# One product for o and v in head groups 2 and 3: seven block products where there were eight

## The chip, the cores and the metric

The kernel runs on one core of a Trainium2 chip. The metric is the device time of one execution in microseconds (us). The core has a matrix engine (TensorE, PE in the profile, with its weight loads as PEld), a vector engine (VectorE, DVE), a scalar engine (ScalarE, ACT), GpSimd (POOL), and SyncE (SP), which here only issues transfers. Each engine works through its own list of instructions in order, and semaphores join the lists.

## The reference, cut to what matters

Two layers work on 256 tokens of 2048 channels; the part below is one layer. Everything is float32.

```python
u = rms_norm(x, norm_g)
p = u @ w_in                                   # 256 x 2048 by 2048 x 12304
qk, v, o, z_a, ig, fg, xb, z_b = split(p)
qk = silu(causal_dwconv(qk, qk_conv))          # a convolution over time, 4 taps
h = mlstm_chunkwise(q, k, v, i_pre, log_f)     # 8 heads of 256
h = h * sigmoid(o);  h = normalise(h) * head_norm_g
y_a = h * silu(z_a)
xc = causal_dwconv(xb, lru_conv_w) + lru_conv_b
y_b = rg_lru(xc) * silu(z_b)                   # gates by two small products, then a scan over time
x = x + concat([y_a, y_b]) @ w_out
```

## The kernel before

**Tiles.** Per layer there are four head groups g of two heads, 512 channels of each kind. The weights lie in memory as units of 1 MB (128 partitions by 2048 float32), in the order in which they are used. A unit has two halves of 128x1024. Each half is split into two numbers of fewer bits, H and L: ScalarE casts it to wH (line 309), VectorE subtracts to get wL (line 310, through the helper at line 178). The activations are kept split in the same way (`x_s`). A float32 product is then three matmuls, HH, HL and LH, which go into one PSUM sum.

- For o, v, z and the output product (`mm_a`, lines 325 to 327) the activation is stationary, a weight row of 512 moves, and a half is 12 matmuls of 512 columns.
- For qk, xb and zb (`mm_b`, lines 342 and 344) the weight is stationary, and a half is 8 matmuls of 512 and 8 of 256 columns.

**Order.** `_sequence()` writes down the order of the units. For a group g from 1 on, it is a head (four units of o, four of v; with zb of group 0 between them in g = 1) and a body: qk, two chunks of the output product of g-1, xb, two more chunks, z, gate, zb. That is 25 units in a body. A running half n prepares (`prepare`) up to half n + `AHEAD` (3), and the pools wH and wL hold four halves (`bufs=4`): so the cast of half n+4 waits until TensorE is done with half n.

**Between the units.** When a PSUM sum is complete, its `..._post` empties it: `evac_b` for qk, xb and zb (a copy on ScalarE, line 416, then an add on VectorE that reads the same sum, line 417), `postfn` of `out_chunk` for the output product (line 799), `o_post`, `v_post`, `z_post`. The rest of the work (convolutions, attention, gates, scan) lies in generators in the queue `bg`, and `pump` hands out some of it after each half. Sums lie in two pairs of PSUM banks, `acc0` and `acc1`, used in turn, so one fills while the other is emptied. Four more banks (`aux0`, `aux1`, two buffers each) serve the small products: attention `ps_S`, `ps_n`, gates `ps_gt`, transposes `ps_ty`. A scheduler in the compiler then shifts instructions inside each engine's list.

**Loading.** `load_unit` takes one buffer of 128x2048 from a pool of three (`wraw`, line 99), and SyncE issues one transfer of 1 MB (line 286) as soon as the buffer's last reader is done.

**What is there but not in use.** The functions `sw_forms`, `sw_chunk` and `sw_post` compute o and v of one group as one product of 2x2 blocks with 7 block products (the Winograd form of Strassen's scheme), in two parts, B (3 block products) and A (4). The set `SW` (line 32) is empty in the kernel before, so none of this runs, and neither does the staging at lines 1033 to 1046 and 1071 to 1077.

Of the kernel before, what the change touches and what calls it, by code (L numbers as in the profile page):

```python
# [9 lines left out]
F32 = mybir.dt.float32  # L10
F32R = mybir.dt.float32r
AF = mybir.ActivationFunctionType
ALU = mybir.AluOpType
# [3 lines left out]
P = 128  # L17
# [11 lines left out]
STAGE_FROM, STAGE_EVERY = 12, 2  # L29


SW = set()
# [6 lines left out]
def _sequence():  # L39


    def units(item):
        return [(item, j) for j in range(_nunits(item))]

    def spread(items, extra):
        groups = []
        for it in items:
            u = units(it)
            groups += [u[i : i + 2] for i in range(0, len(u), 2)]
        side = [x for it in extra for x in units(it)]  # L50
# [24 lines left out]
    return seq  # L75
# [18 lines left out]
def tile_trunk(ctx, tc, x, xt, par, gw, gb, ws, final_g, out):  # L94
# [4 lines left out]
    wraw = ctx.enter_context(tc.tile_pool(name="wraw", bufs=3))  # L99
# [77 lines left out]
    def tt_(o, a, b, op):  # L177
        return V.tensor_tensor(out=o, in0=a, in1=b, op=op)  # L178
# [75 lines left out]
    seq, blocks, pq = _sequence(), _blocks(), {}  # L254

    def sw_blocks(item, kp):

        u = [ws[blocks[("in", item[1], k, item[2]), kp // 2]] for k in "ov"]
        o = 1024 * (kp % 2)
        return [[w[:, o + 512 * r : o + 512 * r + 512] for w in u] for r in range(2)]  # L260

    def load_unit(n, item, j):
        raw = wraw.tile([P, 2048], F32, tag="raw", name="raw")
        st["nload"] += 1
        u = blocks.get((item, j))
        if item[0] == "swB":
            even, odd = sw_blocks(item, j)
            nc.sync.dma_start(out=raw[:, 0:512], in_=even[0])
            nc.sync.dma_start(out=raw[:, 512:1024], in_=odd[1])
            nc.sync.dma_start(out=raw[:, 1024:1536], in_=pq[item[1:]][j][:, 0:512])  # L270
            return raw
        if item[0] == "swA":
            uo = blocks[("in", item[1], "o", item[2]), j // 2]
            nc.sync.dma_start(out=raw[:, 0:1024], in_=ws[uo][:, 1024 * (j % 2) : 1024 * (j % 2) + 1024])
            nc.sync.dma_start(out=raw[:, 1024:1536], in_=pq[item[1:]][j][:, 512:1024])
            tt_(raw[:, 0:512], raw[:, 0:512], raw[:, 1024:1536], ALU.add)
            tt_(raw[:, 1536:2048], raw[:, 0:512], raw[:, 512:1024], ALU.add)
            return raw
        if n < 4:
            w = 512 if n == 0 else 1024  # L280
            for o in range(0, 2048, w):
                if o % 1024 == 0:
                    load_xt(n, o // 1024)
                nc.sync.dma_start(out=raw[:, o : o + w], in_=ws[u][:, o : o + w])
        else:
            nc.sync.dma_start(out=raw, in_=ws[u])
        return raw
# [6 lines left out]
    def prepare(hf):  # L294
        n = len(xT_parts) if hf["i"] == 0 else 1
        if hf["i"] == 0:
            hf["box"]["raw"] = load_unit(n, *hf["at"])
            if n < 4:
                split_xT(0, n, xT_parts[n], range(4 * n, 4 * n + 4))
            if 4 <= st["nload"] < 8:  # L300
                load_x(st["nload"] - 4)
        r = hf["box"]["raw"][:, 1024 * hf["i"] : 1024 * hf["i"] + 1024]
# [235 lines left out]
    def v_post(l, g, acc):  # L538
# [12 lines left out]
        bg.append(e_gen(l, g))  # L551
# [307 lines left out]
    def sw_chunk(l, g, which):  # L859
# [14 lines left out]
        for kp in range(8):  # L874
# [6 lines left out]
            add_unit(mms, before=sw_banks if kp == 0 else None,  # L881
                     after=(lambda: sw_post(l, g, which)) if kp == 7 else None,
                     width=(1024, 512 if which == "B" else 1024))

    def sw_post(l, g, which):
        m = st["sw"]["banks"]
        st["sw"] = None
        if which == "B":
# [4 lines left out]
            st["credit"] -= 1.3  # L893
            return
        require(("lru", l, g - 1))
        require(("ybT", l, g - 1))
        e = st["swe"]
        t = work.tile([P, 512], F32, tag="sC", name="swt")
        tt_(t, e[:, 0, :], m[1], ALU.add)
        tt_(e[:, 0, :], e[:, 0, :], m[0], ALU.add)  # L900
        tt_(e[:, 1, :], e[:, 1, :], m[1], ALU.subtract)
        tt_(e[:, 2, :], e[:, 2, :], m[1], ALU.subtract)
        tt_(t, t, m[2], ALU.add)
        tt_(e[:, 1, :], e[:, 1, :], m[2], ALU.subtract)
        tt_(t, t, m[3], ALU.add)
        st["credit"] -= 4.8
        o_post(l, g, (e[:, 0, :], t))
        v_post(l, g, (e[:, 2, :], e[:, 1, :]))
# [9 lines left out]
    def emit_in(l, kind, g):  # L918
        def first_gen(acc):
# [15 lines left out]
            if SW:  # L935
                yield from sw_forms(l)

        posts = {"o": o_post, "v": v_post, "qk": qk_post, "xb": xb_post, "z": z_post, "zb": zb_post}
# [94 lines left out]
    staged = []  # L1033
    for item, j in seq:
        if item[0] == "swB":
            d = dram.tile([P, 1024], F32, name=f"pq{item[1]}{item[2]}{j}")
            pq.setdefault(item[1:], []).append(d)
            staged.append((d, sw_blocks(item, j)))

    def stage_copy(d, b):  # L1040
        for h in range(2):
            S.dma_start(out=d[:, 512 * h : 512 * h + 512], in_=b[0][1])

    def stage_add(d, b):
        for h in range(2):
            G.dma_start(out=d[:, 512 * h : 512 * h + 512], in_=b[h][h], accum_op=ALU.add)

# [19 lines left out]
    for n, hf in enumerate(order_):  # L1067
# [3 lines left out]
        if hf["i"] == 0:  # L1071
            k = (n // 2 - STAGE_FROM) // STAGE_EVERY
            if n // 2 >= STAGE_FROM and (n // 2 - STAGE_FROM) % STAGE_EVERY == 0:
                if k < len(staged):
                    stage_copy(*staged[k])
                if 0 < k <= len(staged):
                    stage_add(*staged[k - 1])
# [103 lines left out]
```

## Time and profile before

| | |
|---|---|
| time, median of 3 runs (lowest to highest) | 1528.44 us (1528.32 to 1528.78) |
| the profiled execution's own time | 1528.54 us |
| its span, first to last instruction | 1526.8 us |
| TensorE busy | 1509.5 us, 99% of the span |
| VectorE busy | 1077.9 us, 71% |
| ScalarE busy | 891.4 us, 58% |
| GpSimd busy | 62.7 us, 4% |
| moved by DMA | 309 MB, 202 GB/s on average |

The page gives for each engine the time in which an instruction of it ran. Matmuls overlap: one is listed with 390 ns, and the next starts 227 ns later. So what a number of matmuls costs is read from the length of a stretch divided by their count, not from the listed durations. In the same way a VectorE instruction may begin a little before the last one ends.

A steady group, from the first matmul of its o to the first matmul of the next group's o, takes 186.53 us (344.41 to 530.94), of which the head is 43.56 us and the body 142.97 us.

### The profile page before, as it was taken

How to read it: one execution, taken by the hardware profiler on the slowest of the kernel's cores; microseconds unless marked ns; L12 is line 12 of the kernel's file. 1: busy time of each engine (PE TensorE's matmuls, PEld its weight loads, DVE VectorE, ACT ScalarE, POOL GpSimd, SP SyncE). 2: the span in 40 equal slices, each digit the busy share in tenths (PEclk: the TensorE clock that was granted, in tenths of full speed). 3: DMA queues.
4: the chain of work that ended last, by engine and by line, in shares of the span. 5: the costliest groups of instructions: out<-in, count | busy, mean ns of one | idle time of the engine just before them, and what ended most of it. 6: DMA issues, size and time to landing. Idle time of an engine off the chain costs nothing.

```text
span 1526.8 us, 19954 instructions
## 1 busy us (share of the span) xinstructions
PE 1509.5 (99%) x7704; PEld 1284.5 (84%) x7704; DVE 1077.9 (71%) x1510; ACT 891.4 (58%) x1151; POOL 62.7 (4%) x136
## 2 busy tenths in 40 slices
PE   8999999999999999999999999999999999999997
PEld 6888888888888888888888888888888888888885
DVE  6887866676666856758658786676857759477584
ACT  6667554574555745548655485555845557455564
POOL 0010100000000000000001010000000000000002
PEclk9999999999999999999999999999999999999999
DMA  9654556755566555775655545566555665566753
GB/s 357 235 190 174 198 188 209 218 177 198 187 220 202 185 193 193 230 241 192 222 191 179 194 172 195 191 203 218 193 193 183 205 219 193 190 198 219 247 202 102
DMA packets 52926, 309.02 MB, mean 202 GB/s; under 512 B 5712, under 2 KB 8288, under 8 KB 19552
## 3 DMA queue, kind: packets, MB, share of 16 engines
q1 hardware_dynamic: 45776, 287.59, 52.0%
q0 software_dynamic: 4448, 15.75, 6.1%
q10 hardware_dynamic: 2608, 4.42, 0.8%
q8 instruction: 60, 0.98, 0.2%
q14 instruction: 34, 0.28, 0.1%
HBM read 288.85 MB, written 18.89 MB: 202 GB/s over the span
## 4 chain that ended last, share of the span: by engine, by line
PE 97%; DVE 1%; ACT 1%; DMA 0%; issue 0%; ACTq 0%; SPq 0%
PE acc L342 23%; PE acc L325 18%; PE acc L327 18%; PE acc L326 18%; PE acc L344 12%; PE ps_gt L693 3%; PE acc_x L976 0%; PE acc L974 0%; PE acc_x L974 0%; PE acc_x L975 0%; PE acc L976 0%; PE acc L975 0%; PE ps_n L524 0%; PE ps_ty L647 0%; PE ps_n L526 0%; PE ps_n L525 0%
## 5 line engine op out<-in xcount | busy, mean ns | idle before, releaser
L178 DVE TENSOR_TENSOR wL<-raw,wH 128x1024 fp32r<-128x1024 f32 (+1 forms) x529 | 645.0, 1222 | 370.5 <-ACT wH L309 369.3
L309 ACT CAST wH<-raw 128x1024 fp32r<-128x1024 f32 (+1 forms) x529 | 554.2, 1050 | 519.6 <-PE acc L327 262.2
L342 PE MATMUL acc<-x_s,wH 128*128 128x512 f32 x1536 | 542.7, 397 | 0.0
L344 PE MATMUL acc<-x_s,wL 128*128 128x256 f32 x1536 | 430.7, 280 | 0.0
L342 PEld LDWEIGHTS acc<-x_s,wH 128*128 128x128 f32 x1536 | 288.4, 188 | 69.0
L325 PE MATMUL acc<-wH,x_s 128*128 128x512 f32 x768 | 300.8, 392 | 6.4 <-ACT wH L309 6.4
L326 PE MATMUL acc<-wL,x_s 128*128 128x512 f32 x768 | 300.1, 391 | 0.0
L327 PE MATMUL acc<-wH,x_s 128*128 128x512 f32 x768 | 300.1, 391 | 0.0
L344 PEld LDWEIGHTS acc<-x_s,wL 128*128 128x128 f32 x1536 | 290.1, 189 | 0.6
L325 PEld LDWEIGHTS acc<-wH,x_s 128*128 128x128 f32 x768 | 144.9, 189 | 36.4 <-ACT wH L309 6.4
L326 PEld LDWEIGHTS acc<-wL,x_s 128*128 128x128 f32 x768 | 144.8, 189 | 30.3 <-DVE wL L178 0.6
L327 PEld LDWEIGHTS acc<-wH,x_s 128*128 128x128 f32 x768 | 144.8, 189 | 29.9
L325 PE MATMUL acc<-wH,ybH 128*128 128x512 f32 x224 | 88.0, 393 | 0.0
L325 PE MATMUL acc<-wH,yaH 128*128 128x512 f32 x224 | 87.5, 391 | 0.0
L327 PE MATMUL acc<-wH,ybL 128*128 128x512 f32 x224 | 87.4, 390 | 0.0
L326 PE MATMUL acc<-wL,yaH 128*128 128x512 f32 x224 | 87.3, 390 | 0.0
L327 PE MATMUL acc<-wH,yaL 128*128 128x512 f32 x224 | 87.3, 390 | 0.0
L326 PE MATMUL acc<-wL,ybH 128*128 128x512 f32 x224 | 87.2, 389 | 0.0
L327 PEld LDWEIGHTS acc<-wH,ybL 128*128 128x128 f32 x224 | 42.0, 188 | 9.1
L327 PEld LDWEIGHTS acc<-wH,yaL 128*128 128x128 f32 x224 | 42.1, 188 | 9.0
L325 PEld LDWEIGHTS acc<-wH,yaH 128*128 128x128 f32 x224 | 42.1, 188 | 8.9
L326 PEld LDWEIGHTS acc<-wL,yaH 128*128 128x128 f32 x224 | 42.1, 188 | 8.3
(189 smaller groups left out, 1432.3 us busy)
## 6 DMA issues: line engine op xcount, KB each, us to landing
raw<-in_ws_dram SPq DMA_DIRECT2D x260, 1024.0 KB, 4.9
x_d<-stage POOLq DMA_DIRECT2D x24, 512.0 KB, 5.3
x_d<-x_acc ACTq DMA_DIRECT2D x8, 512.0 KB, 8.1
x_acc<-x_d SPq DMA_DIRECT2D x8, 512.0 KB, 5.5
raw<-in_ws_dram SPq DMA_DIRECT2D x6, 512.0 KB, 7.8
xp<-in_xt_dram SPq DMA_DIRECT2D x8, 256.0 KB, 7.0
x_acc<-in_x_dram SPq DMA_DIRECT2D x4, 512.0 KB, 9.2
nb<-nG_d POOLq DMA_DIRECT2D x8, 256.0 KB, 4.3
```

The lines of the kernel that those rows point to most:

```text
L178: return V.tensor_tensor(out=o, in0=a, in1=b, op=op)
L309: S.copy(out=H[:, o : o + w], in_=r[:, o : o + w])
L325: PE.matmul(ps[:, t, :], a_H[:, kt, tsl], Hv[:, k, :], start=s, stop=False)
L326: PE.matmul(ps[:, t, :], a_H[:, kt, tsl], Lv[:, k, :], start=False, stop=False)
L327: PE.matmul(ps[:, t, :], a_L[:, kt, tsl], Hv[:, k, :], start=False, stop=e)
L342: PE.matmul(ps[:, ct, :], Hv[:, k, csl], xs[:, kt].rearrange("p a t -> p (a t)"), start=s, stop=False, skip_group_check=True)
L344: PE.matmul(ps[:, ct, T : 2 * T], Lv[:, k, csl], xs[:, kt, 0, :], start=False, stop=e, skip_group_check=True)
L693: PE.matmul(o, W[:, ib, jl], xs[:, ib, a, :], start=j == 0 and i == 0 and W is Hv and a == 0, stop=i == 1 and W is Lv, skip_group_check=True)
```

## The change

`SW` now holds groups 2 and 3 of both layers. Their heads (o and v, eight units) are gone from the sequence. In their place, parts B and A of group g+1 are laid between the units of the body of group g (g = 1 and 2), as eight units each: the body has thirteen groups (pairs of units, and gate alone); `spread` puts B's units, one or two at a time, behind the first six and A's behind the other seven.

The blocks: the tokens are cut in two (t = 0, 1), the 2048 input channels into even and odd blocks of 128, and the 1024 columns into o and v. With weights wo and wv (even and odd rows), part B needs wo even, wv odd and the sum wo even + wv even; part A needs wo odd and three sums (wv even + wv odd, that plus wo even, and that plus wo odd). Each B unit is 9 matmuls of 512 columns (6 in its first half, 3 in its second, whose weights are 128x512), each A unit 12. All sums of weight blocks are made on VectorE in the raw buffers before they are split: one of 128x512 for a B unit, three for an A unit. The activations' four block sums (the tile `sf`) are made once a layer by `sf_forms` at the end of `first_gen`, behind the gate scores of group 0; `sf` lies where `x_acc` lies at other times. While a part runs (`st["sw"]`), its sums hold one pair of `acc` and both buffers of `aux0`, so the body's sums use one pair only, and the small products the two buffers of `aux1`. When a part is complete, `sw_post` empties it; it is now a generator in `bg` and does so in steps. For part A these are seven VectorE adds, after which `o_post`, `v_post` and `e_gen` follow. The raw pool is now 7 buffers of 128x1024, and each half is loaded by a transfer of its own (512 KB).

```diff
@@ -26,10 +26,9 @@
-STAGE_FROM, STAGE_EVERY = 12, 2
-SW = set()
+SW = {(l, g) for l in range(DEPTH) for g in (2, 3)}
@@ -47,13 +46,15 @@
-        side = [x for it in extra for x in units(it)]
-        seq, k = [], 0
-        for i, grp in enumerate(groups):
-            upto = round((i + 1) * len(side) / len(groups))
-            seq += grp + side[k:upto]
-            k = upto
-        return seq
+        seq, at = [], 0
+        for it, n in extra:
+            side, k = units(it), 0
+            for i, grp in enumerate(groups[at : at + n]):
+                upto = round((i + 1) * len(side) / n)
+                seq += grp + side[k:upto]
+                k = upto
+            at += n
+        return seq + [x for grp in groups[at:] for x in grp]
@@ -64,7 +65,7 @@
-            side = [("swB", l, g + 1), ("swA", l, g + 1)] if (l, g + 1) in SW else []
+            side = [(("swB", l, g + 1), 6), (("swA", l, g + 1), 7)] if (l, g + 1) in SW else []
@@ -96,7 +97,7 @@
-    wraw = ctx.enter_context(tc.tile_pool(name="wraw", bufs=3))
+    wraw = ctx.enter_context(tc.tile_pool(name="wraw", bufs=7))
@@ -251,40 +252,48 @@
-    def load_unit(n, item, j):
...
+    def sw_load(raw, item, kp):
+
+        wo, wv = [ws[blocks[("in", item[1], k, item[2]), kp // 2]] for k in "ov"]
+        o = 1024 * (kp % 2)
+        even, odd = slice(o, o + 512), slice(o + 512, o + 1024)
+        r, q = raw
         if item[0] == "swB":
...
+            nc.sync.dma_start(out=r[:, 0:512], in_=wo[:, even])
+            nc.sync.dma_start(out=q[:, 0:512], in_=wv[:, even])
+            nc.sync.dma_start(out=r[:, 512:1024], in_=wv[:, odd])
+            tt_(q[:, 0:512], q[:, 0:512], r[:, 0:512], ALU.add)
         else:
-            nc.sync.dma_start(out=raw, in_=ws[u])
-        return raw
+            nc.sync.dma_start(out=q, in_=wv[:, o : o + 1024])
+            nc.sync.dma_start(out=r, in_=wo[:, o : o + 1024])
+            tt_(q[:, 0:512], q[:, 0:512], q[:, 512:1024], ALU.add)
+            tt_(r[:, 0:512], r[:, 0:512], q[:, 0:512], ALU.add)
+            tt_(q[:, 512:1024], r[:, 0:512], r[:, 512:1024], ALU.add)
...
+        if u >= 4:
+            box.setdefault("raw", []).append(new_raw())
+            nc.sync.dma_start(out=box["raw"][i], in_=ws[u][:, 1024 * i : 1024 * i + 1024])
...
@@ -878,34 +887,48 @@
-            add_unit(mms, before=sw_banks if kp == 0 else None,
-                     after=(lambda: sw_post(l, g, which)) if kp == 7 else None,
+            add_unit(mms, before=sw_start(l, g, which) if kp == 0 else None,
+                     after=(lambda: bg.append(sw_post(l, g, which))) if kp == 7 else None,
                      width=(1024, 512 if which == "B" else 1024))
...
     def sw_post(l, g, which):
         m = st["sw"]["banks"]
-        st["sw"] = None
         if which == "B":
             e = st["swe"] = act.tile([P, 3, 512], F32, tag="swe", name="swe")
             S.copy(out=e[:, 0, :], in_=m[0])
             tt_(e[:, 1, :], m[1], e[:, 0, :], ALU.subtract)
             tt_(e[:, 2, :], m[2], e[:, 1, :], ALU.add)
-            st["credit"] -= 1.3
-            return
...
+            yield 1.3
+        else:
+            e = st["swe"]
+            t = work.tile([P, 512], F32, tag="sC", name="swt")
+            tt_(e[:, 2, :], e[:, 2, :], m[1], ALU.subtract)
+            tt_(t, e[:, 0, :], m[1], ALU.add)
+            yield 1.3
+            tt_(e[:, 0, :], e[:, 0, :], m[0], ALU.add)
+            tt_(e[:, 1, :], e[:, 1, :], m[1], ALU.subtract)
+            yield 1.3
+            tt_(t, t, m[2], ALU.add)
+            tt_(e[:, 1, :], e[:, 1, :], m[2], ALU.subtract)
+            yield 1.3
+            tt_(t, t, m[3], ALU.add)
+            o_post(l, g, (e[:, 0, :], t))
+            yield 0.7
+            v_post(l, g, (e[:, 2, :], e[:, 1, :]))
+            yield 1.5
+        st["sw"] = None
+        st["sw" + which, l, g] = True
+        if which == "A":
+            yield from e_gen(l, g)
...
@@ -932,10 +955,13 @@
             yield from gates_tr(l)
-            if SW:
-                yield from sw_forms(l)
+            yield from sw_forms(l)
```

Three places in the lists show how instructions move. The first is TensorE's list in group 1 of the first layer, between the two sums of qk (`acc` is the body's sum, `sacc` with or without a number the sums of a part, `x_s` the split activations). Before, the matmuls of the second sum follow directly on the first:

```order
L344 MATMUL acc<-x_s,wL 128x256
L342 MATMUL acc<-x_s,wH 128x512
L344 MATMUL acc<-x_s,wL 128x256
L342 MATMUL acc<-x_s,wH 128x512
L344 MATMUL acc<-x_s,wL 128x256
L342 MATMUL acc<-x_s,wH 128x512
```

and now one unit of B stands between them:

```order
L354 MATMUL acc<-x_s,wL 128x256
L864 MATMUL sacc<-wH,x_s 128x512
L865 MATMUL sacc<-wL,x_s 128x512
L866 MATMUL sacc<-wH,x_s 128x512
L864 MATMUL sacc_2072<-wH,sf 128x512
L865 MATMUL sacc_2072<-wL,sf 128x512
L866 MATMUL sacc_2072<-wH,sf 128x512
L864 MATMUL sacc<-wH,sf 128x512
L865 MATMUL sacc<-wL,sf 128x512
L866 MATMUL sacc<-wH,sf 128x512
L352 MATMUL acc<-x_s,wH 128x512
```

Nine matmuls of B lie between the last of one sum and the first of the next, which now goes into the same pair of banks.

The second place is VectorE's list at the end of group 1 of the first layer, behind its last sum of zb. `xc<-a` is the scan, `swe` and `swt` are what part A's sums are added into, `raw<-raw` is a sum of weight blocks. Before, the next rows are the rest of zb and the splits of the head of group 2:

```order
L178 TENSOR_TENSOR zb<-zb,rb 128x512
L178 TENSOR_TENSOR wL<-raw,wH 128x1024
L178 TENSOR_TENSOR zb<-zsg,xc 128x512
L178 TENSOR_TENSOR wL<-raw,wH 128x1024
L178 TENSOR_TENSOR ybL<-zb,ybH 128x512
L178 TENSOR_TENSOR zsg<-zb,zsg 128x512
L178 TENSOR_TENSOR zb<-zsg,xc 128x512
L178 TENSOR_TENSOR wL<-raw,wH 128x1024
L178 TENSOR_TENSOR ybL<-zb,ybH 128x512
L178 TENSOR_TENSOR wL<-raw,wH 128x1024 x12
```

Now qk of group 2 follows, with B of group 3 and the emptying of A:

```order
L179 TENSOR_TENSOR raw<-raw 128x512
L179 TENSOR_TENSOR wL<-raw,wH 128x1024
L179 TENSOR_TENSOR ybL<-zb,ybH 128x512
L179 TENSOR_TENSOR swe<-swe,sacc 128x512 x2
L179 TENSOR_TENSOR wL<-raw,wH 128x512
L179 TENSOR_TENSOR wL<-raw,wH 128x1024
L179 TENSOR_TENSOR padt<-padt,acc 128x2x256
L179 TENSOR_TENSOR wL<-raw,wH 128x1024
L179 TENSOR_TENSOR padt<-padt,rb 128x2x256
L179 TENSOR_TENSOR swt<-swt,sacc_2909 128x512
L179 TENSOR_TENSOR swe<-swe,sacc_2909 128x512
L179 TENSOR_TENSOR swt<-swt,sacc_2910 128x512
```

The run of twelve splits with nothing between them is gone, and the sums, the emptying of A and the emptying of qk's first sum (`padt<-padt,acc`) share that stretch.

The third place is ScalarE's list at the first place, from the second half of qk's first sum on. `padt<-acc` is the copy that empties this sum; before:

```order
L309 CAST wH<-raw 128x1024 x4
L416 COPY padt<-acc 128x2x256
L309 CAST wH<-raw 128x1024
L408 ACTIVATE qc<-padt,pars 128x256 x2
L309 CAST wH<-raw 128x1024
```

and now, with the casts of B's two halves (1024 and 512 wide) among the others:

```order
L319 CAST wH<-raw 128x1024
L319 CAST wH<-raw 128x512
L319 CAST wH<-raw 128x1024 x2
L426 COPY padt<-acc 128x2x256
L319 CAST wH<-raw 128x1024 x2
L418 ACTIVATE qc<-padt,pars 128x256 x2
```

The copy's place has not moved: the cast just ahead of it is still that of the fourth half behind the one that completes the sum, and two of the three halves between are now B's. On VectorE the add `padt<-padt,acc` likewise stands behind the split of that fourth half.

More of the change, by code (lines that the diff above doesn't have):

```diff
@@ L253, in tile_trunk @@
     halves = []
[L254 to L258 removed]
+    seq, blocks = _sequence(), _blocks()
+    def sw_load(raw, item, kp):
+        wo, wv = [ws[blocks[("in", item[1], k, item[2]), kp // 2]] for k in "ov"]
         o = 1024 * (kp % 2)
[L260 to L287 removed]
@@ new lines, in new_raw, with load @@
+    def new_raw():
+        return wraw.tile([P, 1024], F32, tag="raw", name="raw")
+    def load(hf):
+        item, j = hf["at"]
+        i, box = hf["i"], hf["box"]
+        if item[0][:2] == "sw":
+            if i == 0:
+                box["raw"] = [new_raw(), new_raw()]
+                sw_load(box["raw"], item, j)
+            return
+        u = blocks[item, j]
+        if u >= 4:
+            box.setdefault("raw", []).append(new_raw())
+            nc.sync.dma_start(out=box["raw"][i], in_=ws[u][:, 1024 * i : 1024 * i + 1024])
+        elif i == 0:
+            box["raw"] = [new_raw(), new_raw()]
+            w = 512 if u == 0 else 1024
+            for h in range(2):
+                load_xt(u, h)
+                for o in range(0, 1024, w):
+                    nc.sync.dma_start(out=box["raw"][h][:, o : o + w], in_=ws[u][:, 1024 * h + o : 1024 * h + o + w])
@@ L892, in sw_post @@
             tt_(e[:, 2, :], m[2], e[:, 1, :], ALU.add)
-            st["credit"] -= 1.3
-            return
[L895 to L908, printed above, removed]
+            yield 1.3
[18 more added lines that the diff above has]
+        st["sw" + which, l, g] = True
+        if which == "A":
+            yield from e_gen(l, g)
     def layer_start(l):
```

37 lines of the change are left out of this document (14 added, 23 removed).

## The prediction

> **What bounds the kernel now.** First the page's busy times and its chain of work that ended last, then what TensorE waited for:
>
> ```profile
> span 1526.8 us, 19954 instructions
> PE 1509.5 (99%) x7704; PEld 1284.5 (84%) x7704; DVE 1077.9 (71%) x1510; ACT 891.4 (58%) x1151; POOL 62.7 (4%) x136
> PE 97%; DVE 1%; ACT 1%; DMA 0%; issue 0%; ACTq 0%; SPq 0%
> ...
> PE acc L325 <- ACT wH L309: 6.4, 1, 6.4
> PE acc L974 <- DVE zb L178: 0.4, 1, 0.4
> ```
>
> TensorE waits once, 6.4 us for the first weights, and then never again until the end. So matmuls are the bound, and fewer of them shorten the kernel as long as the others keep ahead. The busy times by stage (body of group 1, head and body of group 2, layer 0):
>
> ```profile
> core 0: us, PE busy (x) PEld busy (x) DVE busy (x) ACT busy (x) POOL busy (x), PEclk, DMA share, GB/s
> 201.43:344.41 142.98, 142.98 (x760) 122.86 (x759) 101.64 (x144) 86.45 (x109) 5.59 (x13) 1.00 0.60 198
> 344.41:387.97 43.56, 43.56 (x195) 36.05 (x193) 26.23 (x28) 20.25 (x22) 0.21 (x2) 1.00 0.56 202
> 387.97:530.94 142.97, 142.97 (x760) 122.86 (x758) 101.68 (x144) 86.43 (x109) 4.90 (x12) 1.00 0.59 197
> ```
>
> VectorE is busy for 71% of a body, 60% of a head: this is the room into which the change moves work.
>
> **What it removes.** The head is 8 units of 24 matmuls: 43.56 / 192 = 0.227 us for one matmul of 512 columns. B and A have 72 + 96 = 168 instead of 192, so 24 × 0.227 = 5.45 us less in a group, **21.8 us** in four. A B unit takes 2.04 us, an A unit 2.72, and a body with both 142.97 + 38.1 = 181.1 us.
>
> **What it adds on VectorE.** The durations by group:
>
> ```profile
> L178 DVE TENSOR_TENSOR wL<-raw,wH 128x1024 fp32r<-128x1024 f32 x527 | 643.6, 1224 | 368.3 <-ACT wH L309 367.1
> L178 DVE TENSOR_TENSOR wL<-raw,wH 128x512 fp32r<-128x512 f32 x2 | 1.4, 692 | 2.2 <-ACT wH L309 2.2
> L178 DVE TENSOR_TENSOR zb<-zsg,xc 128x512 f32<-128x512 f32 x16 | 11.0, 690 | 0.3
> L181 DVE SCALAR_TENSOR_TENSOR x_s<-xp,pars,x_s 128x256 fp32r<-128x256 f32 x16 | 7.0, 480 | 3.5 <-ACT x_s L774 3.4
> L737 DVE TENSOR_TENSOR_SCAN xc<-a,gate 128x256 f32<-128x256 f32 x32 | 20.1, 673 | 0.0
> L612 DVE RECIPROCAL sd<-sd 128x4 f32<-128x4 f32 x8 | 1.4, 178 | 13.3 <-ACT sd L611 13.3
> ...
> 4.35 0.88 DVE L181 SCALAR_TENSOR_TENSOR x_s<-xp,pars,x_s 128x256 fp32r<-128x256 f32 x2 [3.41 <-ACT x_s L774]
> ```
>
> A group's parts need 24 splits of 1024 (29.4 us), 8 of 512 (5.5), 32 block sums (22.1) and 9 adds that empty the banks (6.2): 63 us, where the head had 26. Two instructions of 480 ns in a row took 0.88 us, so the second starts 0.08 early; for some 75 added ones that is 6 us back. VectorE then has 101.7 + 57 = 159 us of work in 181: **88%**. The average fits. What matters is whether each split is ready in time, since it can run only four halves ahead (the four buffers of wL).
>
> **The single pair of sums** is the first price. In a body with a part, a new sum needs the pair that the last one filled, and between them lies only a B unit (2.04), an A unit (2.72) or two. The emptying of qk's first sum, in group 2 before:
>
> ```profile
> 399.14 0.28 PE L344 MATMUL acc<-x_s,wL 128*128 128x256 f32 x1
> 399.26 0.40 PE L342 MATMUL acc<-x_s,wH 128*128 128x512 f32 x1
> ...
> 399.34 1.05 ACT L309 CAST wH<-raw 128x1024 fp32r<-128x1024 f32 x1 [1.73 <-PE acc L342]
> 400.30 0.58 ACT L416 COPY padt<-acc 128x512 f32<-128x512 f32 x1
> ...
> 400.43 1.22 DVE L178 TENSOR_TENSOR wL<-raw,wH 128x1024 fp32r<-128x1024 f32 x1 [1.55 <-ACT wH L309]
> 401.57 0.68 DVE L178 TENSOR_TENSOR padt<-padt,acc 128x512 f32<-128x512 f32 x1
> ...
> 457.50 0.40 PE L325 MATMUL acc<-wH,yaH 128*128 128x512 f32 x1
> 530.94 0.39 PE L325 MATMUL acc<-wH,x_s 128*128 128x512 f32 x1
> ...
> 459.92 0.69 DVE L178 TENSOR_TENSOR padt<-padt,acc 128x512 f32<-128x512 f32 x1
> 533.98 0.68 DVE L178 TENSOR_TENSOR zb<-zb,acc 128x512 f32<-128x512 f32 x1
> L799 ACT COPY stage<-acc 128x1024 f32<-128x1024 f32 x24 | 24.3, 1012 | 26.5 <-PE acc L327 26.5
> ```
>
> The sum is complete at 399.26, and the pair is free at 402.25: 2.99 us, a cast and a split among them. Today nobody needs it for 11 us. The changed lists keep this order (front part, third place), so behind qk's first sum, with one B unit, TensorE waits 2.99 - 2.04 = 0.95. Behind xb's second the emptying takes 460.61 - 457.50 = 3.11, with one B unit: 1.07. Behind zb's second 534.66 - 530.94 = 3.72, the scan in front of it, with one A unit: 1.00. qk's second and xb's first have two B units, an output chunk takes one copy of 1.0 us, z has A units and the gate behind it: nothing. Together 3.0 us in a stage, **12.0** in four. Below, 4, if a shorter wait for the casts lets the copy pass sooner; above, 20, if a busier VectorE adds one split (1.2 us) to half of the twelve.
>
> **VectorE late for a split.** I count along its new list from one split to another. From qk's first half in group 2 to the first half of the output chunk behind qk there are 12 splits of 1024, 3 of 512, 24 adds or products of 512 (A's emptying, zb, block sums), 4 scans, 2 of vL, 6 steps of the convolution: 40.3 us, less 51 × 0.08 = 36.1, and 1.05 for the cast ahead. TensorE gives it, from the end of the fourth half before to the start of the last, 1 half of zb, 8 of qk, 1 A and 3 B units: 9 × 2.82 (11.29 / 4) + 2.7 + 6.1 = 34.2. It is 2.9 us short, of which 1.95 is in the waits above. From the B units inside xb to the first half of the output chunk behind xb, 40 instructions come to 21.7 us, less 3.3, with the cast 19.4, and the wait for the square root is 13.3 / 8 = 1.7 more; TensorE gives 6 B halves (6.1), 4 of xb (11.3) and 15 attention products of some 0.115: 19.1. It is 2.0 short, 1.07 counted. Such a count holds only if VectorE never idles, so I take about twice the uncounted 1.9 and a little for group 1: 4.5 a layer, **9** in both. Bounds 0 (the square root falls elsewhere) and 20 (the 2.9 in every stage, and 2 more).
>
> **The small products** have two banks instead of four. The third of the gate's four sums needs the first one's sigmoids:
>
> ```profile
> 502.17 0.40 PE L693 MATMUL ps_gt<-xcs,wH 128*128 128x256 f32 x2
> 504.47 1.57 ACT L698 ACTIVATE gate<-ps_gt,pars 128x256 f32<-128x256 f32 x4
> ```
>
> They end at about 505.3, the third sum would start at 502.17 + 2.8 = 505.0: 0.3 to 0.5 a stage, **1.5** in all (0 to 3). **The activation sums** add 4 × (1.2 + 4 × 0.4 + 1.2) = 16 us of VectorE a layer beside group 0, and are spread there between splits. At the start TensorE hangs on VectorE:
>
> ```profile
> 12.11 0.29 PEld L326 LDWEIGHTS acc<-wL,x_s 128*128 128x128 f32 x1 [0.20 <-DVE wL L178]
> 8.16 0.63 PE L325 MATMUL acc<-wH,x_s 128*128 128x512 f32 x1
> 8.59 0.63 PE L326 MATMUL acc<-wL,x_s 128*128 128x512 f32 x1
> 13.14 0.39 PE L326 MATMUL acc<-wL,x_s 128*128 128x512 f32 x1
> 13.37 0.40 PE L327 MATMUL acc<-wH,x_s 128*128 128x512 f32 x1
> ```
>
> Some 4 us of them stand among the first splits, and cost **1.5** (0 to 4). ScalarE (86 + 33 of 181 us) has room. **Loads:** 6 MB more in a group, 198 to 237 GB/s, and block sums that need the raw weights two to four splits earlier; **1** (0 to 8).
>
> **Sum** against the profiled execution, 1528.5 (its span 1526.8 and 1.7 around it; the runs' median is 1528.4): 1528.5 - 21.8 + 12.0 + 9 + 1.5 + 1.5 + 1 = **1531.7**, say 1532. The waits eat the gain and a little more.
>
> **Rivals.**
> *The waits are absorbed* (faster). A stall gives VectorE time, so it comes to the next place early, and the counts above overlap. With the pair's wait at 8 of 12 and nothing else but 1: 1516. For it speaks that VectorE is at 71% now and no split of it was ever late after the start; against it that the pair's 2.99 us are measured at an idle VectorE.
> *The block sums wait for transfers* (slower by more). A raw buffer is free seven halves ahead; less the four of the split's lead, the sums have some 7 us beside A units.
>
> ```profile
> raw<-in_ws_dram SPq DMA_DIRECT2D x260, 1024.0 KB, 4.9
> raw<-in_ws_dram SPq DMA_DIRECT2D x6, 512.0 KB, 7.8
> ```
>
> A megabyte lands in 4.9 us; 512 KB took 7.8 when the queue was full at the start. If the latter holds, VectorE stands 0.5 us at each of 32 A units: 1532 + 16 = 1548. The Trainium skill, DMA: Bandwidth & Descriptors, § Bandwidth, advises transfers of at least 1 MiB, which speaks against halving them; by its fit in § Anatomy of one DMA, 2.0 us and the bytes at 436 GB/s, an estimate for 512 KB is 3.2 us, and then this rival decides nothing.
> *The clock drops.* At 8.16 matmuls follow at 0.43 us, at 13.14 at 0.23: after the idle start TensorE ran at half speed for 6 us, at a cost of 2.8. Should each of eight longest stalls (about 3 us) bring that back: 1532 + 22 = 1554. The Trainium skill, TensorE: Matmul & The Clock Gate, § HAM oscillation, puts the limit at an idle gap of about 3.4 us, so by it stalls of 3 us change nothing; that the start is slow agrees.
> That the change doesn't take effect is out: TensorE's list is shorter by 96 matmuls and holds the parts.
>
> **Numbers.** The forecast (1526 to 1540) 0.48, absorbed waits (1510 to 1525) 0.34, transfers 0.13, clock 0.05. Three runs can tell no less than about 0.2%, 3 us. The forecast's share splits into 0.21 within 3 us and 0.27 slower: faster 0.34, same 0.21, slower 0.45. Range 1512 to 1550: from the pair's wait at its lower bound with the rest at 1 to 2, to VectorE at its upper one with the transfers' 8.
>
> **What will show it.** TensorE's waits: on VectorE's `padt` and `zb` about 1 us each, at qk's first, xb's second and zb's second sum, twelve in all; on `wL` behind qk and xb of group 2. A body with parts of 184 to 188 us, not 181. VectorE at 84 to 90% there, its wait for wH shrunk. Wrong it is if TensorE's waits stay under 15 us (absorbed), if `raw` waits for DMA come to over 5 us, or if the granted clock falls below 1.0 in a stage.

## The result and the profile after

The changed kernel takes **1581.53 us** (median of 4 runs, 1576.71 to 1582.95) against 1528.61 us for the kernel before: 1.034 times as long, 95% interval 1.0318 to 1.0363. The prediction was 1532, with a range up to 1550. The page of the changed kernel begins:

```profile
span 1581.2 us, 21173 instructions
...
PE 1511.4 (96%) x7608; PEld 1264.1 (80%) x7608; DVE 1245.5 (79%) x1786; ACT 946.6 (60%) x1226; POOL 62.1 (4%) x136
```

The 96 matmuls are gone, yet TensorE's busy time did not fall, and 70 us of the span are idle where there were 17. The busy time hides part of the loss: a matmul is listed with 390 ns where the next can start after 227, so the first 0.16 us of every wait counts as busy, and so do matmuls at a lower clock. VectorE is at 79%, so it is not full. The stretches say where the time went. The rows are, in this order: group 0 of layer 0; layer 0's bodies of group 1 and 2 (with parts) and of group 3; the same three of layer 1. The columns are those of the table by stage in the prediction.

```profile
6.67:142.75 136.08, 132.05 (x659) 110.96 (x659) 115.05 (x208) 83.56 (x119) 5.04 (x12) 0.99 0.72 248
207.30:402.73 195.43, 185.41 (x928) 153.04 (x926) 153.12 (x212) 116.60 (x144) 5.56 (x13) 1.00 0.70 219
402.73:599.36 196.63, 186.11 (x927) 153.15 (x927) 162.51 (x229) 118.56 (x149) 5.09 (x14) 1.00 0.70 220
599.36:744.52 145.16, 142.89 (x758) 122.84 (x759) 110.66 (x156) 86.93 (x112) 4.37 (x11) 1.00 0.69 214
983.14:1179.98 196.84, 186.90 (x927) 154.07 (x925) 152.94 (x212) 116.80 (x144) 5.53 (x13) 0.99 0.69 218
1179.98:1379.47 199.49, 186.51 (x927) 153.28 (x927) 162.54 (x229) 118.40 (x149) 5.10 (x14) 1.00 0.69 217
1379.47:1526.17 146.70, 144.43 (x759) 124.06 (x759) 110.72 (x156) 86.92 (x112) 4.73 (x10) 0.99 0.67 213
```

Against 181.1 us of matmuls, the four bodies with parts are 14.3, 15.5, 15.7 and 18.4 us too long, 64.0 together. Group 3's bodies lost 2.2 and 3.7 against 143.0. Group 0 of layer 0 takes 136.1, where it took 128.8: 7.3. The heads of group 1 in layer 0 gave 1.7 back. With the 21.8 us saved, that is 53.7; the profiled executions differ by 54.4.

What VectorE waited for (engine, line and tile; releaser; us in total, times, longest):

```profile
DVE raw L179 <- DMA raw<-in_ws_dram: 110.8, 54, 5.3
```

The group of the block sums (busy us, mean ns, idle us in front of it):

```profile
L179 DVE TENSOR_TENSOR raw<-raw 128x512 f32<-128x512 f32 x128 | 88.1, 691 | 111.2 <-DMA raw<-in_ws_dram 110.8
```

Before, VectorE never waited for a weight transfer. Now it stands for 111 us in front of block sums, and everything behind them in its list stands too. One case from the timeline of all engines, in order of time (start, duration, engine, line; beginning of xb's second sum in group 1):

```profile
278.19 1.23 DVE L179 TENSOR_TENSOR wL<-raw,wH 128x1024 fp32r<-128x1024 f32 x1 [2.58 <-ACT wH L319]
...
279.43 1.05 ACT L319 CAST wH<-raw 128x1024 fp32r<-128x1024 f32 x1 [0.27 <-ACT padt L426]
...
279.44 0.33 SPq L265 DMA_DIRECT2D raw<-in_ws_dram  x1
...
283.13 0.69 DVE L179 TENSOR_TENSOR raw<-raw 128x512 f32<-128x512 f32 x1 [1.60 <-DMA raw<-in_ws_dram]
...
284.20 1.22 DVE L179 TENSOR_TENSOR wL<-raw,wH 128x1024 fp32r<-128x1024 f32 x1
...
285.47 0.39 PE L354 MATMUL acc<-x_s,wL 128*128 128x256 f32 x1 [2.44 <-DVE wL L179]
```

A split ends at 279.42 and frees a raw buffer; the load into it is issued at 279.44 and lands 3.7 us later, at 283.11. VectorE had reached the sum that waits for it 1.6 us before. The sum of a B unit that needs it stands four splits ahead of its own in VectorE's list. The split of another half, whose cast was done at 280.5, comes behind it at 284.20, and TensorE waits 2.44 us for that split. No instruction in this chain is slow: the order is wrong.

In the changed kernel's list one can count how many splits stand between a sum and its own split. 32 of the 128 sums stand at their own place, 12 stand 1 or 2 splits ahead, 26 stand 3 ahead and 58 stand 4 to 6 ahead. The idle time in front of those 58 is 99 us, in front of the 32 it is 0. The Trainium skill, Perfetto Trace Analysis, § Per-engine timelines, calls VectorE's queue a strict FIFO; this chain agrees.

TensorE's waits (its direct releasers) show what this became:

```profile
PE acc L352 <- DVE padt L179: 7.9, 6, 2.3
PE sacc L865 <- DVE wL L179: 7.8, 13, 2.0
PE acc L335 <- DVE padt L179: 7.7, 5, 3.4
PE acc L352 <- DVE zb L179: 7.4, 8, 1.2
PE acc L354 <- DVE wL L179: 5.9, 7, 2.4
PE acc L336 <- DVE wL L179: 5.1, 6, 1.7
```

### The profile page after: what moved, and what is told of

Its sections match the earlier page's. It is cut to its first block, busy times and chain, and to the rows that moved or that the text cites. A ratio compares the mean times of both kernels' runs of the same rounds, so it can differ in the third digit from the quotient of the medians.

```text
span 1581.2 us, 21173 instructions
## 1 busy us (share of the span) xinstructions
PE 1511.4 (96%) x7608; PEld 1264.1 (80%) x7608; DVE 1245.5 (79%) x1786; ACT 946.6 (60%) x1226; POOL 62.1 (4%) x136
## 5 line engine op out<-in xcount | busy, mean ns | idle before, releaser
L319 ACT CAST wH<-raw 128x1024 fp32r<-128x1024 f32 (+1 forms) x593 | 599.1, 1026 | 453.1 <-PE acc L337 179.9
L179 DVE TENSOR_TENSOR wL<-raw,wH 128x1024 fp32r<-128x1024 f32 (+1 forms) x593 | 698.2, 1191 | 159.8 <-ACT wH L319 159.2
L335 PE MATMUL acc<-wH,x_s 128*128 128x512 f32 x512 | 201.7, 394 | 10.1 <-ACT wH L319 6.7
L336 PE MATMUL acc<-wL,x_s 128*128 128x512 f32 x512 | 201.7, 394 | 4.4 <-DVE wL L179 4.4
L337 PE MATMUL acc<-wH,x_s 128*128 128x512 f32 x512 | 201.3, 393 | 0.0
L179 DVE TENSOR_TENSOR raw<-raw 128x512 f32<-128x512 f32 x128 | 88.1, 691 | 111.2 <-DMA raw<-in_ws_dram 110.8
L335 PEld LDWEIGHTS acc<-wH,x_s 128*128 128x128 f32 x512 | 97.1, 190 | 30.4 <-ACT wH L319 6.7
L336 PEld LDWEIGHTS acc<-wL,x_s 128*128 128x128 f32 x512 | 97.0, 190 | 26.9 <-DVE wL L179 7.3
L337 PEld LDWEIGHTS acc<-wH,x_s 128*128 128x128 f32 x512 | 97.0, 190 | 19.8
L865 PE MATMUL sacc<-wL,sf 128*128 128x512 f32 x128 | 52.2, 408 | 7.8 <-DVE wL L179 7.8
L864 PE MATMUL sacc<-wH,sf 128*128 128x512 f32 x128 | 50.6, 398 | 3.7 <-ACT wH L319 3.7
```

The costliest lines, as they stand in the source:

```text
L319: S.copy(out=H[:, o : o + w], in_=r[:, o : o + w])
L335: PE.matmul(ps[:, t, :], a_H[:, kt, tsl], Hv[:, k, :], start=s, stop=False)
L336: PE.matmul(ps[:, t, :], a_H[:, kt, tsl], Lv[:, k, :], start=False, stop=False)
L337: PE.matmul(ps[:, t, :], a_L[:, kt, tsl], Hv[:, k, :], start=False, stop=e)
L864: PE.matmul(bank, aH, H, start=first, stop=False)
L865: PE.matmul(bank, aH, L, start=False, stop=False)
```

## The experiments

Theory A: the block sums wait for transfers in front of other work. Theory B: VectorE has too much to do. Rivals for the rest: the halved loads themselves, the single pair of sums, the activation sums (forms). All times are medians; the kernel before took 1528.4 to 1528.8 beside them.

**1. Loads and forms without parts.**

```diff
-SW = {(l, g) for l in range(DEPTH) for g in (2, 3)}
+SW = set()
```

> SW is empty, the loads stay halved (7 buffers of 512 KB) and the activations' block sums (sf_forms) stay. Groups 2 and 3 have their heads again. Theory A (the parts' block sums wait for transfers): halved loads cost nothing by themselves, 1528 to 1530, plus what the forms cost in group 0 of layer 0 (its length was 128.8 before and 136.1 in the changed kernel), so 1529 to 1537. If small transfers were the cost by themselves: over 1545, with TensorE waiting for casts all over the span.

1533.94 us, ratio 1.0038 (1.0023 to 1.0053). Group 0 of layer 0, and a head and body of group 2 and 3 (186.53 before):

```profile
6.56:141.41 134.85, 131.40 (x659) 110.46 (x660) 115.07 (x208) 83.55 (x119) 5.05 (x12) 0.99 0.72 249
392.49:579.03 186.54, 186.54 (x952) 158.91 (x951) 127.84 (x171) 106.61 (x131) 5.10 (x14) 1.00 0.64 197
```

Where no part runs, halved loads cost nothing. Most of the 5.3 us stands in group 0 of layer 0, where the forms run: it takes 6.1 us more than before, and the heads behind it give 1.7 back. Run 9, which moves the forms, brings it back to 128.9.

**2. Block sums on resident data.**

```diff
-            tt_(q[:, 0:512], q[:, 0:512], r[:, 0:512], ALU.add)
+            idle_add(1)   # tt_(scr, x2, x2, ALU.add), x2 from x_s; three of them in an A unit
```

> Every block sum stays on VectorE, with the same size and count and at the same place, but reads resident activations and writes a spare tile, so it waits for no transfer; the split takes the raw blocks as they were loaded (the output is then another). Three columns of the tile swe are one here, to make room. Theory A (VectorE stands 111 us at sums whose weights have not landed, and the splits behind come late): those waits are gone, and the four bodies with parts fall from 195 to 200 us to 184 to 188; 1535 to 1548. Theory B (VectorE simply has too much to do in a body with parts, and the wait for transfers falls into time it would idle): within 4 us of 1581.

1542.52 us; the bodies with parts take 185.4 to 186.1. That is the number theory A gave, but the run proves less than was meant: with nothing to wait for, the 64 sums of a layer stand ahead of its bodies with parts (layer 0's between 5.0 and 215.8 us, layer 1's between 754.5 and 947.7), so VectorE lost their work in the bodies too:

```profile
394.27:580.36 186.09, 183.53 (x927) 153.65 (x927) 144.63 (x197) 118.06 (x150) 5.11 (x14) 1.00 0.74 233
```

144.6 us of VectorE and 197 instructions, where the changed kernel has 162.5 and 229. The sums together with their waits cost some 39 us; A and B stay open.

**3. Block sums on GpSimd.**

```diff
-            tt_(q[:, 0:512], q[:, 0:512], r[:, 0:512], ALU.add)
+            g_(q[:, 0:512], q[:, 0:512], r[:, 0:512], ALU.add)   # G.tensor_tensor; A's three too
```

> The 128 block sums go to GpSimd (its add of 128x512 took 1.34 us in the kernel before, VectorE's 0.69). VectorE loses 88 us of work and the 111 us of waiting in front of it. Theory A and theory B both say faster than 1581: A 1540 to 1555, B 1550 to 1565. If both are wrong and the price is the pair of sums: 1570 or more. The sums come 2 us later at an A unit, which takes back some of it.

1581.26 us: no gain, against both theories. The groups of GpSimd, and VectorE's splits:

```profile
L182 POOL TENSOR_TENSOR raw<-raw 128x512 f32<-128x512 f32 x128 | 229.9, 1799 | 438.2 <-DMA raw<-in_ws_dram 220.0 <-issue 111.1 <-DVE wL L179 47.1
...
L179 DVE TENSOR_TENSOR wL<-raw,wH 128x1024 fp32r<-128x1024 f32 x559 | 734.3, 1327 | 228.3 <-ACT wH L322 224.9 <-DMA raw<-in_ws_dram 2.4
```

An add took 1.80 us, not 1.34, and the splits beside it 1.33 on average, not 1.22. Near z of group 1 nine sums ran in a row for 16.4 us. VectorE gets slower: a cost of its own in place of the old one. TensorE waited only 3.5 us for casts and splits of the parts, but 20.7 us for `padt` and 10.2 for `zb`, the adds with which VectorE empties sums (15.6 and 7.4 in the changed kernel). The run doesn't tell A from B.

**4. Eight raw buffers.**

```diff
-    wraw = ctx.enter_context(tc.tile_pool(name="wraw", bufs=7))
+    wraw = ctx.enter_context(tc.tile_pool(name="wraw", bufs=8))
-            e = st["swe"] = act.tile([P, 3, 512], F32, tag="swe", name="swe")
+            e = st["swe"] = act.tile([P, 1, 512], F32, tag="swe", name="swe")   # e[:, 0] for all three
```

> One more raw buffer, 8 for 7, room for it made by letting the three columns of swe be one (the sums of o and v then overwrite each other). Every load may start one half earlier: 1.4 us beside an A unit, 2.8 us elsewhere. Theory A: the waits for raw fall from 111 us to 40 to 70, the time to 1555 to 1570. Theory B: 1578 to 1583.

1581.33 us, and the wait hardly moved:

```profile
DVE raw L179 <- DMA raw<-in_ws_dram: 101.9, 57, 5.0
```

A miss for theory A as it was put. But in this kernel's list 74 of the 96 sums of A stand 4 to 6 splits ahead (42 before), and 18 of B's 32 stand 5 ahead. So the lead that the buffer gave was used up by the new places in the list. Why the scheduler moved the sums up (it may reckon with the earlier loads) no run shows. This suggests that not the lead of the loads decides, but where a sum stands in the list; runs 5 and 6 test it.

**5 and 6. The sums held back in VectorE's list.** An ordering without a semaphore: a sum stands behind the split of the half before its unit (5), or two splits earlier (6).

```diff
+    def hold(ins):
+        order(ins, splits[-1])          # 6: splits[-3]
...
-            tt_(q[:, 0:512], q[:, 0:512], r[:, 0:512], ALU.add)
+            hold(tt_(q[:, 0:512], q[:, 0:512], r[:, 0:512], ALU.add))   # and A's three
```

> Only the order of VectorE's list is changed: each block sum stands behind the split of the half before its own unit, where the program writes it; in the changed kernel most stand 3 to 6 splits ahead of their own. Theory A, sharpened by the run with eight buffers (there the sums stood 4 to 6 splits ahead, and waited 102 us): not the lead of the loads but the place of the sums in the list is the cause. The waits for raw fall from 111 us to under 15, the bodies with parts to 185 to 188 us, the time to 1540 to 1550. Rival C (the transfers are too slow as such, 219 GB/s in 512 KB pieces): the wait moves to ScalarE's cast and the time stays over 1570.

> The same with two more splits of lead: a sum stands behind the split three halves before its unit. Theory A: a load has 4 splits of time between the freeing of its buffer and the sum, some 7 to 11 us, and lands in 4.9 to 7.6: waits for raw of 10 to 40 us, 1542 to 1560. Rival C: over 1570.

1561.34 and **1543.58** us. VectorE's idle time in front of all 128 sums is 1.2 and 1.0 us, where it was 111.2. The three bodies of layer 0, held by one and then by three:

```profile
205.22:396.48 191.26, 183.46 (x928) 153.66 (x926) 156.46 (x215) 116.45 (x144) 5.67 (x14) 1.00 0.69 223
396.48:587.88 191.40, 184.31 (x927) 153.79 (x927) 164.33 (x229) 118.43 (x149) 5.80 (x14) 1.00 0.70 226
587.88:735.25 147.37, 144.45 (x759) 124.04 (x759) 109.73 (x154) 86.53 (x112) 4.26 (x10) 0.99 0.68 211
```

```profile
207.11:394.01 186.90, 182.43 (x928) 153.77 (x926) 153.44 (x211) 116.09 (x144) 5.56 (x13) 1.00 0.71 227
394.01:581.82 187.81, 184.18 (x926) 153.98 (x927) 163.87 (x229) 117.69 (x149) 5.80 (x14) 1.00 0.73 232
581.82:727.18 145.36, 142.89 (x758) 122.75 (x759) 111.17 (x157) 87.39 (x112) 4.37 (x11) 1.00 0.69 214
```

This separates A from B. In run 6 VectorE has the same work in a body (153.4 and 163.9 us, as in the changed kernel) in 9 us less. Only the order differs, and 38 us are gone. (The hold moved the sums, and with them a few others: some 96% of VectorE's other instructions keep their order.) Theory B falls, and so does rival C: the transfers were fast enough. Run 5 shows the other side, and missed its 1540 to 1550: a sum held until it is next in line delays its own cast and split. TensorE's waits for casts and splits of the parts (`sacc`) are 7.5 us there and gone in run 6, and the bodies are 4 us longer than in run 6.

**7 and 8. Copy first.** The emptying copy stands ahead of the next cast, its add ahead of that cast's split; in 7 alone, in 8 with sums behind the split two halves before.

```diff
+            if "evac" in st:
+                ec, ea = st.pop("evac")     # evac_b's copy and add
+                order(c, ec)                # c, d: cast and split of the next half
+                order(d, ea)
```

> The sums stay where they are; for qk, xb and zb the copy that empties a PSUM pair stands ahead of the next cast on ScalarE, and the add behind it ahead of that cast's split on VectorE. The prediction put 12 us on these waits. If they are a price of their own: 1567 to 1573. If TensorE waits there mostly because VectorE stands at a sum: 1573 to 1583.

> Both: sums behind the split two halves before their unit, and the copy first. Theory A with the pair's waits as predicted: 1540 to 1548 less 8 to 12 is 1528 to 1540. If the pair's waits only change their name (a cast or split that stands behind the copy is late by the same time): 1540 to 1550.

1572.51 and **1537.36** us: 9.0 less than the changed kernel, and 6.2 less than run 6. The sums in run 6 may stand one split further ahead, so the 6.2 is not the copy's alone. The three bodies of layer 0 in run 8:

```profile
204.32:387.80 183.48, 181.72 (x928) 154.08 (x927) 153.14 (x212) 114.88 (x143) 5.57 (x13) 1.00 0.73 231
387.80:575.84 188.04, 183.46 (x928) 154.03 (x927) 164.19 (x230) 117.80 (x148) 5.51 (x14) 1.00 0.73 231
575.84:723.21 147.37, 144.28 (x760) 123.94 (x759) 111.81 (x157) 87.34 (x112) 4.37 (x11) 0.99 0.68 212
```

The body of group 1 is now within 2.4 us of its matmuls; the bodies that follow a part are not. At the start of group 3, part A's sums still hold the other pair, and no part lies between qk's two sums: TensorE waits 3.1 us there.

**9 to 12. The remaining costs.** Run 9: `sf_forms` behind group 0's gates, and the gate's third and fourth sum in the pair that z left. Run 10: part A over six groups of units, with `o_post` and `v_post` put off behind zb. Runs 11 and 12: part A over seven again, `swt` in another buffer, its emptying at the front of the queue `bg`, with `o_post` and `v_post` behind it; 12 with the gate's banks, 11 without.

```diff
+            if g == 0:                      # end of gate_post, runs 9 to 12
+                yield from sw_forms(l)
...
-            yield from sw_forms(l)          # end of first_gen, runs 9 to 12
...
+                ps = gate_acc[:, b, :] if gate_acc is not None else aux("ps_gt")   # 9, 10, 12
...
-            side = [(("swB", l, g + 1), 6), (("swA", l, g + 1), 7)] if (l, g + 1) in SW else []
+            side = [(("swB", l, g + 1), 6), (("swA", l, g + 1), 6)] if (l, g + 1) in SW else []   # 10
...
-                     after=(lambda: bg.append(sw_post(l, g, which))) if kp == 7 else None,
+                     after=(lambda: bg.appendleft(sw_post(l, g, which))) if kp == 7 else None,   # 11, 12
-            t = work.tile([P, 512], F32, tag="sC", name="swt")
+            t = act.tile([P, 2, 512], F32, tag="stage", name="swt")[:, 0, :]   # 11, 12
```

> On top of the sums behind the split two halves before and the copy first: the activations' block sums (sf_forms) run behind the gates of group 0, under the heads of group 1, not among group 0's body; and the gate's third and fourth sum use the pair of acc that z has left, so the gate has four banks. The first should give back what group 0 of layer 0 lost (133.5 against 128.8 us: 4 to 5), the second the 1.3 us wait for the first sigmoids and what hangs on it, four times (5 to 9): 1537.4 less 9 to 14 is 1523 to 1528. If the gate's matmuls wait for z's emptying in the pair instead: 1530 to 1534.

> The same, and part A over six groups of the body, not seven, so its sums are emptied before the next group's qk starts, and qk has the pair to itself; o_post and v_post stay behind zb. The wait of 3.1 us at qk's second sum of group 3 and the 1 to 2 us at that of group 2 should go (8 to 10 us in all), against a denser A (VectorE): 1515 to 1523 if A's VectorE work fits, 1525 to 1532 if splits are late beside the denser A.

> Sums behind the split two halves before, copy first, forms behind group 0's gates, the gate with two banks again; and a part's emptying (sw_post) goes to the front of the queue bg, so that its pair is free before the next group's qk needs a second one; o_post and v_post follow behind zb's work. The first four make about 1537 less 7, that is 1530 by the run with the gate's banks, in which group 3's body took 146.4 us against 143.0 and group 2's 186.9 against 183.9. If both differences come from the late emptying, 4 x 3 us less: 1518 to 1523, faster than both kernels. If the adds at the front make splits late instead: 1528 to 1535.

> The same with the gate's third and fourth sums in the pair of acc that z left. In the run before this call the bodies of group 1 took 183.9 us with these banks and 183.5 without: the wait only moved from the third sum to zb's first. So within 2 us of the run without them; if the banks help once the rest is in place, 4 to 8 us less.

Run 9: 1529.28 us, ratio 1.0003 (0.9994 to 1.0013), above what was expected. Group 0 fell from 133.5 us in run 8 to 128.9, so the forms gave their share back; the bodies of group 1 stayed at 183.9 (183.5 and 183.7 in run 8), so the gate's banks gave nothing there.

Run 10: 1556.00, a miss. TensorE now stood 5.9 to 6.1 us before qk in four places. The lists show why. Since the program empties part A before qk begins, qk's first sum goes into the pair that A held, and the adds that empty A stand behind the scan and among zb's work on VectorE:

```profile
382.78 2.43 DVE L757 TENSOR_TENSOR_SCAN xc<-a,gate 128x256 f32<-128x256 f32 x4
...
391.04 0.68 DVE L179 TENSOR_TENSOR swe<-swe,sacc 128x512 f32<-128x512 f32 x1
...
391.87 0.76 PE L362 MATMUL acc<-x_s,wH 128*128 128x512 f32 x1 [6.14 <-ACT zsg L780]
```

The add at 391.04 is the fourth of seven and the last that reads this pair. In all four places qk's first matmul starts 0.15 us after its end. The profile names ScalarE's sigmoid of zb, which ended in between; qk's sum does not need it.

Run 11: 1524.88, ratio 0.9976 (0.9965 to 0.9987), just above its 1518 to 1523. Run 12: **1522.98 us, ratio 0.9963 (0.9949 to 0.9977)**, 0.4% faster than the kernel before and within 2 us of run 11. Its group 0 and three bodies of layer 0:

```profile
6.67:135.55 128.88, 128.81 (x658) 109.23 (x659) 102.89 (x188) 81.77 (x119) 5.80 (x12) 1.00 0.74 256
201.77:385.65 183.88, 182.40 (x927) 154.40 (x926) 159.17 (x223) 116.85 (x145) 5.68 (x14) 1.00 0.73 232
385.65:572.39 186.74, 183.61 (x928) 154.24 (x926) 164.32 (x230) 118.19 (x148) 5.09 (x14) 1.00 0.72 233
572.39:715.23 142.84, 142.84 (x760) 122.82 (x759) 110.93 (x156) 87.38 (x112) 4.26 (x10) 1.00 0.69 217
```

Group 0 and group 3 are back at 128.9 and 142.8. The four bodies with parts are still 2.8, 5.6, 2.6 and 5.5 us over 181.1, 16.5 together; with the 21.8 saved that leaves 5.3, about what the medians show (5.6).

## Why the prediction was wrong

**The failed step is the term "Loads: 1 (0 to 8)".** It cost 38 us (1581.5 less run 6, which has the same instructions in another order), and `raw`'s waits for DMA, a sign against the forecast from 5 us on, came to 110.8. The prediction had the fact that the sums "need the raw weights two to four splits earlier". It then priced the wait as if a sum stood at its own split ("the sums have some 7 us"), and left 1 us for all that stands behind a waiting sum. For a sum four splits further ahead, only one or two splits lie between the freeing of its buffer and the sum: in the case shown above VectorE reached the sum 2.1 us after the buffer was free, and the load took 3.7. The rival on transfers named the right cause, at 16 us for A's sums only, with a chance of 0.13. B's sums, which it left out, carry 42 of the 111 us. Its mechanism was not quite right either: it asked whether 512 KB lands in 4.9 or 7.8 us. They land in 4.9, as the megabyte did:

```profile
raw<-in_ws_dram SPq DMA_DIRECT2D x526, 512.0 KB, 4.9
```

Run 6 works with the same transfers. The rule of the Trainium skill, DMA: Bandwidth & Descriptors, § Bandwidth, on transfers of at least 1 MiB decided nothing here. The fit in § Anatomy of one DMA of the same page of the Trainium skill, from which the prediction estimated 3.2 us, is given there for transfers issued by GpSimd; these, issued by SyncE, took 4.9, and the measurement decides.

**What it removes, 21.8 us:** right; the sums over the stages close to 1 us with it.

**VectorE 88% busy, the average fits:** right. Run 6 has 163.9 of 187.8 us in group 2's body, 87%, and 153.4 of 186.9 in group 1's, 82%; the bodies are 186.9 and 187.8 us, inside the 184 to 188 that the prediction named.

**The single pair, 12.0 us:** the mechanism is right, the size too high. In run 6, where no sum stands in the way, TensorE's waits at the three places come to 7.2 us in ten waits: 2.8 behind qk's first sum, 2.9 behind xb's second (in group 1 alone), 1.5 behind zb's second. Copy first brought 9.0 us on the changed kernel and 6.2, with the hold one split shorter, against run 6. Where A still holds the pair at qk of group 3, the prediction put nothing; in run 6 group 3's bodies are 2.4 and 2.6 us too long, and emptying first (run 12) takes this away.

**VectorE late for a split, 9 us:** too high. With the sums held, these TensorE waits of run 6 are left on splits and on the gate:

```profile
PE ps_gt L707 <- ACT gate L712: 5.2, 4, 1.3
...
PE acc L341 <- DVE wL L179: 1.3, 3, 0.6
```

1.3 us on splits, near the lower bound of 0. **The small products, 1.5 us:** too low; the gate's third sum waits 1.3 us, not 0.3 to 0.5, four times: 5.2. **The forms, 1.5 us (0 to 4):** too low; 5.3 by run 1, above the bound. In the changed kernel they made TensorE wait 3.4 us for the emptying of xb's second sum in group 0, which stood behind VectorE's other work, and matmuls at half speed followed.

**The clock:** the rival of eight drops did not come, but three did. Seven matmuls at half speed follow a gap of 3.45 us in group 0, and five or ten follow gaps of 2.0 and 2.3 us in layer 1; at some 0.2 us for each slow matmul of 512 columns and 0.1 for one of 256, an estimate of 4 us in all, of which 1.4 lies in group 0, within what the forms cost.

Without the loads' term the forecast would still have been 12 us low (run 6 against 1532). By stage: run 6's four bodies with parts are 24.9 us over their matmuls, where the prediction's terms came to 23.5; group 3's bodies are 5.0 over, where it had nothing; group 0 and 1's heads in layer 0 are 5.5 over, where it had 1.5. So the bodies came out near right by luck, with terms that were not: what the pair and the late splits did not take went to the gate and to waits that these runs do not take apart.

## What to carry to other kernels

An instruction that waits for a transfer delays all that stands behind it in its engine's list; read in the list how far ahead of its use it stands, and compare that with when its buffer comes free, not with how many buffers there are. In run 4 one more buffer moved such instructions further up in the list and gained nothing, so hold them by an explicit order, early enough for their own user (run 5 was too late) and late enough for their load. Work laid into idle slots is worth its saving only after each small price around it (who holds a PSUM pair, which list the emptying stands in, where one-time work falls) has been taken out one by one.

## What the runs showed of the hardware

**Half clock after short gaps.** Twice in the changed kernel TensorE waits 2.27 us at qk's second sum of group 3. In layer 0 nothing follows:

```profile
613.19 0.50 PE L352 MATMUL acc<-x_s,wH 128*128 128x512 f32 x1 [2.27 <-DVE padt L179]
613.53 0.28 PE L354 MATMUL acc<-x_s,wL 128*128 128x256 f32 x1
613.64 0.40 PE L352 MATMUL acc<-x_s,wH 128*128 128x512 f32 x1
613.88 0.28 PE L354 MATMUL acc<-x_s,wL 128*128 128x256 f32 x1
```

In layer 1 the matmuls from 1394.15 on come at 0.43 and 0.21 us, twice the time:

```profile
1393.30 0.50 PE L352 MATMUL acc<-x_s,wH 128*128 128x512 f32 x1 [2.27 <-DVE padt L179]
...
1394.15 0.63 PE L352 MATMUL acc<-x_s,wH 128*128 128x512 f32 x1
1394.58 0.41 PE L354 MATMUL acc<-x_s,wL 128*128 128x256 f32 x1
1394.79 0.63 PE L352 MATMUL acc<-x_s,wH 128*128 128x512 f32 x1
```

The Trainium skill, TensorE: Matmul & The Clock Gate, § HAM oscillation, warns of gaps above about 3.4 us; these are shorter, and the measurement decides. What differs between the two layers no run shows: in both, the last wait before the gap was one of 0.63 us, 13.8 us earlier. The same page of the Trainium skill, § A second HAM failure mode, tells of a kernel whose clock fell and rose under frequent short idling; here no other wait lies in the 13 us before the gap, so this trace does not show that case. In run 10 eight matmuls at half speed (0.43 us) follow a wait of only 1.40 us, at 495.46, with no other wait over 0.3 us in the 100 us before it.

**GpSimd and VectorE slow each other.** In run 3 the block sums of 128x512 took 1.80 us on GpSimd (its six adds of this shape at the end of the same kernel 1.34), and the splits in the body of group 1 took 1.40 us:

```profile
L179 DVE TENSOR_TENSOR wL<-raw,wH 128x1024 fp32r<-128x1024 f32 x72 | 99.7, 1404 | 31.0 <-ACT wH L322 28.3 <-DMA raw<-in_ws_dram 2.4
...
L179 DVE TENSOR_TENSOR padt<-padt,rb 128x512 f32<-128x512 f32 x4 | 4.9, 1234 | 0.0
...
L179 DVE TENSOR_TENSOR padt<-padt,acc 128x512 f32<-128x512 f32 x4 | 2.7, 679 | 0.0
```

The product with both operands in SBUF (`padt`, `rb`) took 1.23 us, where it took 0.69 in the changed kernel; the add that reads one operand from PSUM kept its 0.68. The Trainium skill, SBUF — State Buffer, § Who interferes with whom, says that a VectorE instruction contends with GpSimd's reads when both its inputs lie in SBUF, and not with one input there; these rows agree.
